# Low halves of attention keys in zero-padded 128-row tiles

## The chip, the cores and the metric

The kernel runs on one core of one Trainium2 chip. The metric is the device time of one execution in microseconds (us); lower is better. Three timed runs of the kernel before gave 2253.48, 2253.60 and 2255.27 us, the median is 2253.6 us.

The engines are called as the profile calls them: PE is the matrix engine (TensorE) and PEld its weight loads, DVE is VectorE, ACT is ScalarE, POOL is GpSimd, SP the engine that issues most DMAs. A matmul has a stationary operand, which a weight load puts into the array, and a moving operand, whose columns stream through it.

## The reference, cut to what matters

The model has two layers over 512 tokens of width 1024. A layer is a feed-forward block, a mixer and a second feed-forward block, all in float32.

```python
for l in range(DEPTH):
    h = h + 0.5 * swiglu(rms_norm(h, ffn1_norm[l]), ...)
    h = h + hybrid_mixer(rms_norm(h, mix_norm[l]), ...)
    h = h + 0.5 * swiglu(rms_norm(h, ffn2_norm[l]), ...)
```

The mixer has three kinds of heads of width 64: four heads of full attention that share two heads of keys and values, six heads of windowed attention with a bias by distance, and six heads of a gated delta rule that runs over the sequence in chunks of 64 tokens. The change touches the scores of the first two kinds, for one head `softmax(q k^T / 8 [+ bias])`, with 512 queries and 512 keys.

## The kernel before, in words

Every float32 matrix product that must be exact enough is split: an operand is rounded to a high half in the format fp32r, the rest is its low half, and products of halves are added up in PSUM. In the feed-forward blocks that is three matmuls of a 128x128 stationary tile with 512 moving columns (`mm3`, lines 214 to 218): high weights with high inputs, high weights with low inputs, low weights with high inputs. The first two have the same stationary operand, and each has its own weight load.

In attention two heads are a pair, called `tile_` in the code; there are five pairs in a layer and four blocks of 128 queries in each, so 20 units per layer. `queries` (line 812) makes for each head of the pair a tile `qs` of 128 rows: the 64 rows of the head's own half hold the high half of its queries, the other 64 rows hold the low half. `keys` (line 822) makes `kh`, in which head `i` has its high half twice, once in each half of the rows, so that one 128-row matmul adds high times high and low times high. The low half of the keys, `kl`, is one tile of 128 rows: rows 0 to 63 belong to the first head and rows 64 to 127 to the second.

`scores` (line 847) issues four matmuls for a unit. Two have the full `qs` block (128 rows) as stationary operand and `kh` as moving operand (line 863). Two have only the 64 rows with the high half of the queries as stationary operand, and 64 rows of `kl` as moving operand (line 865). DVE then finds the row minimum or maximum (with the bias added where there is one, line 876), ACT takes the exponential (line 873 or 878), DVE the reciprocal of the sum (line 879), and POOL scales the probabilities (line 880). `weigh` (line 884) runs one unit later: PE turns the probabilities (`ppt`, line 890, 128 rows and 128 columns of weights), ACT copies them (line 892), and PE multiplies them with the values (`pav`, line 896, 128 rows and 64 columns).

The scan of the delta rule is interleaved with the first fifteen units; its matmuls have 64-row or 64-column stationary operands (`pkq` line 685, `prr` line 697, `pS` line 707, `po` line 720). After unit 15 `delta_finish` (line 920) puts a run of small DVE operations beside the last units, and the output projection (`pwo`) begins between them.

The order of instructions on each engine is not that of the code alone: the kernel is built with a scheduler that orders them by its own model of their times, so an edit can move instructions it doesn't name. Each engine then runs its own list strictly in order, and waits on semaphores.

Memory of the attention pool lies on that of pools that were closed before. `delta_solve` and `project_groups` come just ahead of attention; `self.last` and `delta_solve` keep POOL busy until shortly before it.

Of the kernel before, what the change touches and what calls it, by code (L numbers as in the profile page):

```python
# [9 lines left out]
F32 = mybir.dt.float32  # L10
F32R = mybir.dt.float32r
# [8 lines left out]
P = 128  # L20
T = 512
# [330 lines left out]
class Mixer:  # L352
# [444 lines left out]
    def attention(self, ap, pp, scan, sp):  # L797
        k, nc, c = self.k, self.nc, self.c
        ident = c["ident"]
        self.mix = [None] * KD  # L800
        low, high = slice(0, 64), slice(64, 128)

        def gain(g, r):
            return g if isinstance(g, float) else g[r]

        def turned(qkv, tl):
            p = pp.tile([P, T], F32, name="pqk", tag="t", bufs=2)
            for t in range(NT):
                nc.tensor.transpose(out=p[:, t * P:t * P + P], in_=qkv[:, t, tl * P:tl * P + P], identity=ident)
            return p  # L810

        def queries(p, g):
            out = []
            for hb, other in ((low, high), (high, low)):
                q = ap.tile([P, T], F32R, name="qs", bufs=4)
                nc.scalar.activation(out=q[hb], in_=p[hb], func=AF.Copy, scale=gain(g, hb))
                nc.vector.scalar_tensor_tensor(out=q[other], in0=p[hb], scalar=gain(g, hb), in1=q[hb],
                                               op0=ALU.mult, op1=ALU.subtract)
                out.append(q)
            return out  # L820

        def keys(p, g):
            kh = ap.tile([P, 2, T], F32R, name="kh", bufs=2)
            kl = ap.tile([P, T], F32R, name="kl", bufs=2)
            for i, hb in enumerate((low, high)):
                for r in (low, high):
                    nc.scalar.activation(out=kh[r, i], in_=p[hb], func=AF.Copy, scale=gain(g, r))
                nc.vector.scalar_tensor_tensor(out=kl[hb], in0=p[hb], scalar=gain(g, hb), in1=kh[hb, i],
                                               op0=ALU.mult, op1=ALU.subtract)
            return kh, kl  # L830

        ops = {}

        def load(i):
            if i < 2:
                if i == 0:
                    kv = keys(turned(self.qkv[0], 2), 1.0), self.qkv[0][:, :, 384:512]
                else:
                    kv = ops[0][1:]
                ops[i] = (queries(turned(self.qkv[0], i), 0.125), *kv)  # L840
            elif i < 5:
                g = self.qkv[i - 1]
                ops[i] = (queries(turned(g, 0), self.gq8), keys(turned(g, 1), self.nbk), g[:, :, 256:384])

        state = {}

        def scores(tile_, t):
            if t == 0:
                state["pv"] = pp.tile([P, T], F32, name="pav", tag="v")
                state["bias"] = []  # L850
                if tile_ >= 2:
                    for h in (2 * tile_ - 4, 2 * tile_ - 3):
                        bias = ap.tile([P, NWIN], F32, name="bias", bufs=BIAS_BUFS)
                        src = k.line[h:h + 1, 0:P * 2 * T].rearrange("o (p n) -> (o p) n", n=2 * T)
                        nc.sync.dma_start(out=bias, in_=src[:, P - 1:P - 1 + NWIN])
                        state["bias"].append(bias)
            if t == LOAD_AT:
                load(tile_ + 1)
            tk = slice(t * P, t * P + P)
            q, (kh, kl), v = ops[tile_]  # L860
            ps = [pp.tile([P, T], F32, name="psc", tag="s", bufs=2) for _ in range(2)]
            for par in range(2):
                nc.tensor.matmul(out=ps[par], lhsT=q[par][:, tk], rhs=kh[:, par], start=True, stop=False)
            for par, hb in enumerate((low, high)):
                nc.tensor.matmul(out=ps[par], lhsT=q[par][hb, tk], rhs=kl[hb], start=False, stop=True)  # L865
            probs = []
            for par in range(2):
                pb = ap.tile([P, T], F32, name="prob", bufs=2 * AHEAD + 2)
                nm = ap.tile([P, 1], F32, name="nm", bufs=2 * AHEAD + 2)
                sm = ap.tile([P, 1], F32, name="sm", bufs=2 * AHEAD + 2)  # L870
                if tile_ < 2:
                    nc.vector.tensor_reduce(out=nm, in_=ps[par], axis=AX, op=ALU.max, negate=True)
                    nc.scalar.activation(out=pb, in_=ps[par], func=AF.Exp, bias=nm, accum_out=sm)
                else:
                    o = T - P - t * P
                    nc.vector.tensor_tensor_reduce(out=pb, in0=ps[par], in1=state["bias"][par][:, o:o + T], scale=1.0,
                                                   scalar=3e38, op0=ALU.add, op1=ALU.min, accum_out=nm)
                    nc.scalar.activation(out=pb, in_=pb, func=AF.Exp, scale=-1.0, bias=nm, accum_out=sm)
                nc.vector.reciprocal(out=sm, in_=sm)  # L879
                nc.gpsimd.tensor_tensor(out=pb, in0=pb, in1=sm.to_broadcast([P, T]), op=ALU.mult)  # L880
                probs.append(pb)
            return probs, state["pv"], v, tile_, t

        def weigh(probs, pv, v, tile_, t):
            tk = slice(t * P, t * P + P)
            turns = []
            for pb in probs:
                pt = pp.tile([P, T], F32, name="ppt", tag="t", bufs=2)
                for kt in range(NT):
                    nc.tensor.transpose(out=pt[:, kt * P:kt * P + P], in_=pb[:, kt * P:kt * P + P], identity=ident)  # L890
                full = ap.tile([P, T], F32, name="pth", bufs=4)
                nc.scalar.activation(out=full, in_=pt, func=AF.Copy)
                turns.append(full)
            for kt in range(NT):
                for hb, full in zip((low, high), turns):
                    nc.tensor.matmul(out=pv[hb, tk], lhsT=v[:, kt, hb], rhs=full[:, kt * P:kt * P + P],  # L896
                                     start=kt == 0, stop=kt == NT - 1)
            if t == NT - 1:
                hi = k.xp.tile([P, T], F32R, name="mxh", tag=f"xh{tile_}")
                lo = k.xp.tile([P, T], F32R, name="mxl", tag=f"xl{tile_}")  # L900
                nc.scalar.activation(out=hi, in_=pv, func=AF.Copy)
                nc.vector.tensor_tensor(out=lo, in0=pv, in1=hi, op=ALU.subtract)
                self.mix[tile_] = hi, lo

        pending = []
        load(0)
        for tile_ in range(5):
            for t in range(NT):
                pending.append(scores(tile_, t))
                if len(pending) > AHEAD:  # L910
                    weigh(*pending.pop(0))
                unit = 4 * tile_ + t
                for _ in range(SCAN_AT.count(unit)):
                    next(scan)
                if unit == FINISH_AT:
                    self.delta_finish(sp)
        for u in pending:
            weigh(*u)
# [136 lines left out]
```

## Time and profile before

| | |
|---|---|
| median of three timed runs | 2253.6 us |
| profiled execution, its span (the profile gives no other time of it) | 2258.2 us |
| PE busy | 2206.7 us, 98% |
| PEld busy | 1749.9 us, 77% |
| DVE busy | 1143.1 us, 51% |
| ACT busy | 789.7 us, 35% |
| POOL busy | 478.3 us, 21% |
| matmuls on line 863 (`kh`) | 80, mean 520 ns |
| matmuls on line 865 (`kl`) | 80, mean 530 ns |
| weight loads of lines 216 and 217, which share the stationary operand | 1408 each, mean 188 ns |

Busy time is the time in which an engine had some instruction under way; matmuls overlap, so the duration of one matmul is longer than the step from its start to the start of the next, and it is this step that says how fast PE gets on. The attention of layer 1 lies between about 590 and 724 us of the span, that of layer 2 between about 1712 and 1838 us. The granted clock of PE (PEclk) is 1.00 at its upper level of 2.4 GHz and 0.50 at 1.2 GHz.

### The profile page before, as it was taken

To read this page: it belongs to the slowest core of one execution; us is meant where nothing else is said; L and a number is where in the kernel's file an instruction comes from. 1 tells how busy PE (TensorE), PEld (TensorE's weight loads), DVE (VectorE), ACT (ScalarE), POOL (GpSimd) and SP (SyncE) were. 2 spreads that over 40 slices of the span, in tenths; PEclk is the share of its full clock that TensorE was granted. 3 is DMA by queue.
4 is the path that set the end of the run, shared out by engine and by line. 5 is a ranking of instruction groups with operands and counts; after the bars stand their busy time and mean duration, and the time that the engine had idled before them with its cause. 6 is when DMAs were issued, how large, how long until landed. Compare 5 with 4: busy or idle time off the path is not lost.

```text
span 2258.2 us, 30283 instructions
## 1 busy us (share of the span) xinstructions
PE 2206.7 (98%) x12212; PEld 1749.9 (77%) x12212; DVE 1143.1 (51%) x1881; ACT 789.7 (35%) x1153; POOL 478.3 (21%) x482
## 2 busy tenths in 40 slices
PE   8999999998999999999999999999989999999999
PEld 5888887778766888888788888877787778888887
DVE  5333334779567443333443333447795765434333
ACT  4222223534465332222332222235335643222221
POOL 3101012207154220101221010123072532101010
PEclk9999999999799999999999999999998999999999
DMA  5432323233202223333232323232341023232333
GB/s 174 123 96 96 97 92 124 75 92 98 57 18 81 92 92 96 94 91 101 85 95 91 102 91 97 91 124 68 100 111 36 28 94 93 94 93 92 95 94 102
DMA packets 93076, 206.82 MB, mean 92 GB/s; under 512 B 38561, under 2 KB 39073, under 8 KB 92936
## 3 DMA queue, kind: packets, MB, share of 16 engines
q1 hardware_dynamic: 91168, 199.98, 29.0%
q10 hardware_dynamic: 1768, 4.91, 0.7%
q8 instruction: 96, 1.57, 0.3%
q14 instruction: 44, 0.36, 0.1%
HBM read 193.83 MB, written 14.18 MB: 92 GB/s over the span
## 4 chain that ended last, share of the span: by engine, by line
PE 89%; DVE 7%; issue 1%; ACT 1%; DMA 1%; SPq 0%; ACTq 0%; DVEq 0%
PE pg L218 14%; PE pg L216 14%; PE pg L217 14%; PE pd L218 7%; PE pd L217 7%; PE pd L216 7%; PE pc L216 2%; PE pav L896 2%; PE ppt L890 2%; PE pc L218 2%; PE pc L217 2%; PE psc L865 1%; PE pkq L685 1%; PE pwo L217 1%; DVE wlo L211 1%
## 5 line engine op out<-in xcount | busy, mean ns | idle before, releaser
L210 ACT ACTIVATE whi<-wraw 128x1024 fp32r<-128x1024 f32 (+3 forms) x344 | 351.3, 1022 | 1225.7 <-PE pg L217 655.3
L216 PE MATMUL pg<-xh,whi 128*128 128x512 f32 x1408 | 558.2, 397 | 8.5 <-ACT xh L236 8.3
L217 PE MATMUL pg<-xl,whi 128*128 128x512 f32 x1408 | 558.7, 397 | 1.6 <-DVE xl L237 1.5
L218 PE MATMUL pg<-xh,wlo 128*128 128x512 f32 x1408 | 558.0, 396 | 0.8 <-DVE wlo L211 0.8
L211 DVE TENSOR_TENSOR wlo<-wraw,whi 128x1024 fp32r<-128x1024 f32 (+3 forms) x344 | 409.1, 1189 | 89.8 <-ACT whi L210 83.4
L296 POOL TENSOR_TENSOR s<-s,rstd 128x512 f32<-128x512 f32 x88 | 152.7, 1737 | 1146.5 <-ACT s L295 1146.5
L216 PEld LDWEIGHTS pg<-xh,whi 128*128 128x128 f32 x1408 | 265.4, 188 | 73.4 <-ACT xh L236 8.3
L217 PEld LDWEIGHTS pg<-xl,whi 128*128 128x128 f32 x1408 | 265.1, 188 | 68.0 <-DVE xl L237 4.8
L218 PEld LDWEIGHTS pg<-xh,wlo 128*128 128x128 f32 x1408 | 265.3, 188 | 65.2 <-DVE wlo L211 1.9
L218 PE MATMUL pd<-hh,wlo 128*128 128x512 f32 x704 | 278.7, 396 | 0.9 <-DVE wlo L211 0.9
L216 PE MATMUL pd<-hh,whi 128*128 128x512 f32 x704 | 278.4, 396 | 0.0
L217 PE MATMUL pd<-hl,whi 128*128 128x512 f32 x704 | 278.4, 395 | 0.0
L310 DVE SCALAR_TENSOR_TENSOR x<-pd,x 128x512 f32<-128x512 f32 x96 | 66.4, 691 | 283.4 <-PE pd L218 283.4
L298 DVE TENSOR_TENSOR h<-pg,s 128x512 f32<-128x512 f32 x88 | 60.8, 691 | 287.9 <-PE pg L218 281.4
L294 DVE TENSOR_TENSOR s<-pg,rstd 128x512 f32<-128x512 f32 x88 | 60.6, 692 | 229.6 <-PE pg L218 229.5
L218 PEld LDWEIGHTS pd<-hh,wlo 128*128 128x128 f32 x704 | 132.3, 188 | 34.0 <-DVE wlo L211 2.2
L217 PEld LDWEIGHTS pd<-hl,whi 128*128 128x128 f32 x704 | 132.3, 188 | 31.9
L216 PEld LDWEIGHTS pd<-hh,whi 128*128 128x128 f32 x704 | 132.4, 188 | 31.8
L880 POOL TENSOR_TENSOR prob<-prob,sm 128x512 f32<-128x512 f32 x80 | 84.3, 1061 | 149.8 <-DVE sm L879 126.3
L753 PE MATMUL pgr<-wlo,xh 128*128 128x384 f32 (+1 forms) x256 | 91.4, 357 | 12.2 <-DVE wlo L211 12.1
L245 POOL TENSOR_TENSOR acc<-acc,sq 128x512 f32<-128x512 f32 x42 | 67.4, 1606 | 132.6 <-ACT sq L244 131.9
L754 PE MATMUL pgr<-whi,xl 128*128 128x384 f32 (+1 forms) x256 | 90.1, 352 | 0.0
(234 smaller groups left out, 2712.8 us busy)
## 6 DMA issues: line engine op xcount, KB each, us to landing
wraw<-in_gu_dram SPq DMA_DIRECT2D x176, 512.0 KB, 3.6
wraw<-in_wd_dram SPq DMA_DIRECT2D x64, 448.0 KB, 3.3
wraw<-in_wd_dram SPq DMA_DIRECT2D x32, 512.0 KB, 3.5
wraw<-in_w_c_dram SPq DMA_DIRECT2D x24, 512.0 KB, 3.6
wraw<-in_w_gb_dram SPq DMA_DIRECT2D x24, 384.0 KB, 3.0
wraw<-in_w_o_dram SPq DMA_DIRECT2D x14, 512.0 KB, 3.6
bias<-line SPq DMA_DIRECT2D x12, 448.0 KB, 4.9
saved<-x SPq DMA_DIRECT2D x16, 256.0 KB, 2.0
```

The lines of the kernel that those rows point to most:

```text
L210: nc.scalar.activation(out=hi, in_=raw, func=AF.Copy)
L211: nc.vector.tensor_tensor(out=lo, in0=raw, in1=hi, op=ALU.subtract)
L216: nc.tensor.matmul(out=out, lhsT=w[0], rhs=x[0], start=first, stop=False)
L217: nc.tensor.matmul(out=out, lhsT=w[0], rhs=x[1], start=False, stop=False)
L218: nc.tensor.matmul(out=out, lhsT=w[1], rhs=x[0], start=False, stop=last)
L245: nc.gpsimd.tensor_tensor(out=n["acc"], in0=n["acc"], in1=sq, op=ALU.add)
L296: nc.gpsimd.tensor_tensor(out=s, in0=s, in1=n["rstd"], op=ALU.mult)
L298: nc.vector.tensor_tensor(out=h, in0=pp[1], in1=s, op=ALU.mult)
L310: nc.vector.scalar_tensor_tensor(out=self.x[dm], in0=p, scalar=0.5, in1=self.x[dm], op0=ALU.mult, op1=ALU.add)
L753: nc.tensor.matmul(out=o, lhsT=xh[:, tk], rhs=lo[:, wc], start=False, stop=False)
L754: nc.tensor.matmul(out=o, lhsT=xl[:, tk], rhs=hi[:, wc], start=False, stop=kk == KD - 1)
L880: nc.gpsimd.tensor_tensor(out=pb, in0=pb, in1=sm.to_broadcast([P, T]), op=ALU.mult)
```

## The change

`kl` becomes a tile of 128 rows for each head, as `kh` is: head `i` writes its low half into the 64 rows where its high queries lie, and the other 64 rows are zero. The matmul on `kl` then takes the full 128-row `qs` block as stationary operand, the same as the matmul on `kh`; the low queries meet the zeros. To write the zeros only once per layer, two such tiles (`pads`) are made at the start of attention, zeroed by four memsets on POOL, and used in turn. Each tile is 4 KB per row, where `kl` had 2 KB.

```diff
+        kept, pads = [], [ap.tile([P, 2, T], F32R, name=f"kl{i}") for i in range(2)]
+        for kl in pads:
+            for i, other in enumerate((high, low)):
+                nc.gpsimd.memset(kl[other, i].bitcast(F32), 0.0)
...
-            kl = ap.tile([P, T], F32R, name="kl", bufs=2)
+            kl = pads[len(kept) % 2]
+            kept.append(kl)
...
-                nc.vector.scalar_tensor_tensor(out=kl[hb], in0=p[hb], scalar=gain(g, hb), in1=kh[hb, i],
+                nc.vector.scalar_tensor_tensor(out=kl[hb, i], in0=p[hb], scalar=gain(g, hb), in1=kh[hb, i],
...
             for par in range(2):
                 nc.tensor.matmul(out=ps[par], lhsT=q[par][:, tk], rhs=kh[:, par], start=True, stop=False)
-            for par, hb in enumerate((low, high)):
-                nc.tensor.matmul(out=ps[par], lhsT=q[par][hb, tk], rhs=kl[hb], start=False, stop=True)
+                nc.tensor.matmul(out=ps[par], lhsT=q[par][:, tk], rhs=kl[:, par], start=False, stop=True)
```

The number of matmuls and weight loads stays as it is. The order moves at a few places. On PE near the end of the attention of layer 1 (`ppt` are turned probabilities, `pwo` the output projection), this stood before:

```order
L890 MATMUL ppt<-consts,prob 128x128 x4
L863 MATMUL psc<-kh,qs 128x512 x2
L896 MATMUL pav<-pth,qkv_4426 64x128
L865 MATMUL psc<-kl,qs 128x512 x2
L890 MATMUL ppt<-consts,prob 128x128 x4
```

and the same stretch has these rows now:

```order
L894 MATMUL ppt<-consts,prob 128x128 x4
L868 MATMUL psc<-kh,qs 128x512
L869 MATMUL psc<-kl_4637,qs 128x512
L216 MATMUL pwo_6223<-mxh,wohi_6218 128x512
L217 MATMUL pwo_6223<-mxl,wohi_6218 128x512
L868 MATMUL psc<-kh,qs 128x512
L869 MATMUL psc<-kl_4637,qs 128x512
L900 MATMUL pav<-pth,qkv_4426 64x128 x7
```

Two `kl` matmuls of 64 rows that stood side by side are apart, each now right behind its `kh` matmul. Before there are three places with two `kl` side by side, now there is none.

On PE at the opening of the attention of layer 2, behind the first `prr` of the scan, this stood before:

```order
L697 MATMUL prr<-vs,Y_11917 64x64
L863 MATMUL psc<-kh,qs 128x512
L865 MATMUL psc<-kl,qs 128x512
L707 MATMUL pS<-vn,kd_12008 64x64 x6
L707 MATMUL pS<-vn,kd_12009 64x64 x6
L720 MATMUL po<-vn,A_11918 64x64
```

and this stands now:

```order
L697 MATMUL prr<-vs,Y_11919 64x64
L707 MATMUL pS<-vn,kd_12010 64x64 x6
L707 MATMUL pS<-vn,kd_12011 64x64 x6
L720 MATMUL po<-vn,A_11920 64x64
L720 MATMUL po<-vn,A_11921 64x64
L720 MATMUL po<-vn,A_11920 64x64
L720 MATMUL po<-vn,A_11921 64x64
L720 MATMUL po<-vn,A_11920 64x64
L868 MATMUL psc<-kh,qs 128x512
L869 MATMUL psc<-kl_13385,qs 128x512
```

The first pair of score matmuls has moved behind the scan's `pS` and part of its `po`; that is the order which layer 1 has in both kernels.

On POOL at the opening of the attention of layer 1, the state of the scan is cleared and scaled (`S`), and the first probabilities follow. Before:

```order
L625 TENSOR_TENSOR yi_3532<-yi_3532,tmp_3534 96x30
L669 MEMSET S 128x768
L713 TENSOR_TENSOR S<-S,lstep 64x6x64 x2
L880 TENSOR_TENSOR prob<-prob,sm 128x512
L713 TENSOR_TENSOR S<-S,lstep 64x6x64 x2
```

and now:

```order
L625 TENSOR_TENSOR yi_3532<-yi_3532,tmp_3534 96x30
L669 MEMSET S 128x768
L713 TENSOR_TENSOR S<-S,lstep 64x6x64 x2
L805 MEMSET kl_4636 64x512 x2
L805 MEMSET kl_4637 64x512 x2
L884 TENSOR_TENSOR prob<-prob,sm 128x512
L713 TENSOR_TENSOR S<-S,lstep 64x6x64 x2
```

The four memsets stand between the scaling of `S` and the first probabilities. The first two wait for DMAs of `delta_solve` whose memory they take; the other two wait for the last `pp` matmul of `delta_solve` (line 658). Only the first two are waited for by the first score matmuls on `kl`. On SP the order of DMAs is unchanged.

## Rows read from the trace of the kernel before

**Rows 1.** The page: the chain of work that ended last, by engine.
```profile
PE 89%; DVE 7%; issue 1%; ACT 1%; DMA 1%; SPq 0%; ACTq 0%; DVEq 0%
```

**Rows 2.** Busy us of each engine by stretch, PEclk, DMA share, GB/s.
```profile
617.00:703.00 86.00, 83.47 (x956) 60.11 (x954) 57.40 (x134) 52.95 (x109) 44.58 (x45) 1.00 0.06 19
703.00:724.00 21.00, 19.54 (x164) 13.32 (x163) 18.47 (x54) 11.77 (x26) 9.12 (x8) 1.00 0.09 26
1818.00:1838.00 20.00, 20.00 (x181) 14.37 (x177) 16.80 (x52) 11.70 (x27) 9.36 (x8) 1.00 0.10 28
```

**Rows 3.** Waits of PE, 590 to 724 us: us in total, times, longest.
```profile
PE pav L896 <- ACT pth L892: 1.3, 1, 1.3
```

**Rows 4.** Line 865 alone by stretch: PE and PEld busy, PEclk, DMA, GB/s.
```profile
586.00:617.00 31.00, 4.75 (x6) 1.71 (x6) 0.50 0.01 2
617.00:703.00 86.00, 13.45 (x28) 4.93 (x28) 1.00 0.06 19
703.00:724.00 21.00, 2.48 (x6) 0.92 (x6) 1.00 0.09 26
1709.00:1726.00 17.00, 2.38 (x3) 0.86 (x3) 0.50 0.00 1
1726.00:1818.00 92.00, 15.90 (x33) 5.85 (x33) 1.00 0.05 17
1818.00:1838.00 20.00, 1.99 (x4) 0.73 (x4) 1.00 0.10 28
```

**Rows 5.** Lines 863 and 865: ns min/median/max, starts; idle before.
```profile
L863 PE MATMUL psc<-kh,qs x80: 387/495/796, 593.5 to 1827.8; 128*128 128x512 f32 x80
...
L865 PE MATMUL psc<-kl,qs x80: 490/498/793, 594.2 to 1828.2; 64*128 64x512 f32 x80
...
  issue: 21.0, 77
```

**Rows 6.** Timeline of PE, 700 to 716 us: start, us, line, tiles, count.
```profile
703.01 0.49 PE L865 MATMUL psc<-kl,qs 64*128 64x512 f32 x2
...
706.70 0.50 PE L865 MATMUL psc<-kl,qs 64*128 64x512 f32 x1
707.13 0.49 PE L863 MATMUL psc<-kh,qs 128*128 128x512 f32 x1
...
708.78 0.39 PE L218 MATMUL pwo<-mxh,wolo 128*128 128x512 f32 x1
709.02 0.39 PE L216 MATMUL pwo<-mxh,wohi 128*128 128x512 f32 x1
...
709.70 0.39 PE L216 MATMUL pwo<-mxh,wohi 128*128 128x512 f32 x1
710.02 1.09 PE L896 MATMUL pav<-pth,qkv 128*64 128x128 f32 x16
711.05 0.50 PE L217 MATMUL pwo<-mxl,wohi 128*128 128x512 f32 x1
711.38 0.39 PE L218 MATMUL pwo<-mxh,wolo 128*128 128x512 f32 x1
```

**Rows 7.** Timeline of weight loads, same stretch, idle time ahead in brackets.
```profile
707.55 0.18 PEld L865 LDWEIGHTS psc<-kl,qs 64*128 64x128 f32 x1 [0.24 <-issue]
...
708.79 0.19 PEld L216 LDWEIGHTS pwo<-mxh,wohi 128*128 128x128 f32 x1
```

**Rows 8.** Timeline, 580 to 606 us, in the low clock.
```profile
598.85 0.79 PE L865 MATMUL psc<-kl,qs 64*128 64x512 f32 x1
...
599.57 1.55 PE L685 MATMUL pkq<-S,kq 128*64 128x128 f32 x8
```

**Rows 9.** Timelines around the opening of attention in layer 1, POOL and PE.
```profile
561.12 0.74 POOL L669 MEMSET S<- 128x768 f32 x1 [5.73 <-ACT xi L631]
...
598.03 1.04 POOL L880 TENSOR_TENSOR prob<-prob,sm 128x512 f32<-128x512 f32 x1 [33.57 <-DVE sm L879]
...
585.96 2.47 PE L658 MATMUL pp<-Y,p1s 32*32 32x32 f32 x48 [0.90 <-ACT p1s L653]
```

## The prediction

> **What bounds the kernel now.** I read the chain of waits first. PE holds 89% of it [rows 1], so what shortens PE's list can shorten the kernel. Then busy time by stretch, for the two stretches in which the change lies. In most of the attention of layer 1 PE is busy for 83.47 of 86 us and DVE for 57.40; in its last 21 us DVE is busy for 18.47, nearly as much as PE's 19.54, and at the end of layer 2 for 16.80 of 20 [rows 2]. Then who waits for whom: over the whole attention of layer 1 PE's longest entry is one wait of 1.3 us for ACT [rows 3], and the list has six entries with 4.7 us in all. So attention is bound by PE, except for its two tails, where a run of small DVE operations could be the limit. Last the timeline of PE and of its weight loads, to see what a step on PE costs. There the reader is to look at starts, not at durations: a `kl` matmul lasts 0.498 us and a `kh` matmul 0.495 us in the median [rows 5], but the step from one start to the next is what counts.
>
> **What a step costs.** Where matmuls of 128 rows and 128 weight columns follow each other, the step is 0.24 us (708.78 to 709.02) [rows 6]; others of that run are 0.23. I take 0.23. When the next one has another form (64 of rows or columns), the step is 0.32 (709.70 to 710.02). The step of the first one behind such a switch is 0.33 (711.05 to 711.38). One between two switches takes both: `kl` to `kh` is 0.43 (706.70 to 707.13) [rows 6]. So a change of form costs 0.09 us on the way in and 0.10 behind it, 0.19 together. The loads show why: the load for 709.02 starts at 708.79, while the matmul of 708.78 runs; the load of a `kl` matmul comes only after 0.24 us in which PEld did nothing [rows 7], and over all `kl` loads that idle time is 21.0 us in 77 places [rows 5]. The number of rows by itself costs nothing: with 64 rows and with 128 the 512 columns take the same time.
>
> The Trainium skill says the same of the switch: in "TensorEngine Tiling (Array Packing)", Key Properties, changing the tiling mode drains the engine. It also holds a rule against the change (Tiling Modes there): two tiles of 64 rows work at once. The trace agrees where two stand side by side: at 703.01 two `kl` matmuls share 0.49 us [rows 6]. By that rule alone, with all 40 units so ordered, padding would cost 40 steps of 0.23, 9.2 us; the order has only three such places, and the sum below goes by these.
>
> **The sum.** Removed:
> - In PE's order before, 77 of the 80 `kl` matmuls stand behind another form (74 of them behind `kh`), the other three behind a `kl`. The switch ahead of each of the 77 goes: 77 x 0.09 = 6.9 us, and the step behind it loses its 0.10: 7.7 us. 14.6 together.
> - 38 of them have a 128x128 matmul next (`kh`, `ppt`, `pqk`, `pwo`), 42 in the new order. The switch back goes as well: 42 x 0.19 = 8.0 us. For the other 38 the next matmul has 64 rows or columns, and that switch stays.
> - Nine of the 80 lie in the low clock [rows 4], where the step of 0.43 is 0.72 (598.85 to 599.57) [rows 8]. At that ratio of 1.67 their share gains 9/80 x 22.6 x 0.67 = 1.7 us more.
>
> Added:
> - Three pairs that ran side by side now take a step each: 3 x 0.23 = 0.7 us.
> - Four memsets per layer on POOL. A memset of 768 columns took 0.74 us; 512 columns are 0.49 in proportion, 2 us for the four. POOL lies idle for 33.57 us ahead of 598.03 [rows 9]. The first two, which the score matmuls wait for, wait for DMAs ahead of that idle time; the second two wait for the `pp` matmuls that end at about 588.4 (585.96 + 2.47) and end some 1 us later, 8 us ahead of POOL's next work. Cost 0 for both layers; without that cover at most the 2 us per layer, and below nothing it can't be.
> - Weight loads: one for each matmul as before. That two matmuls share a stationary operand saves none; the FFN's pairs with the same weights have one load each as well.
> - DVE writes the same number of columns for `kl`. A padded tile of zeros streams the same 512 columns.
>
> So PE's list gets 14.6 + 8.0 + 1.7 - 0.7 = 23.6 us shorter, about 24.
>
> What of it shows in the time? Ten of the 80 `kl` matmuls lie in the two tails [rows 4], where DVE is nearly as full as PE [rows 2]; I take nothing there, which leaves 70/80, 21 us. In the rest PE would be 21 us faster over some 225 us, so waits for DVE, ACT and POOL that now end early enough will sometimes end last: `ppt` for POOL's probabilities, `pkq` and `pS` for the scan on DVE, `kh` and `qs` at the start of a pair of heads. The bound is from no such loss (21 us) to half (10 us). As PE waits so little now [rows 3] I take a fifth, 4 us. Then 17 us remain.
>
> The profiled span of 2258.2 us is 4.6 us, 0.2%, longer than the median of the timed runs; I take the difference over unchanged: 2253.6 - 17 = 2236.6, say 2237 us.
>
> **The clock.** It falls to the low level ahead of both attentions, while PE runs short matmuls of 32 rows with gaps, and rises again in them: 31 us at 0.50 in layer 1, 17 us in layer 2 [rows 4]. One us at the low level does the work of 0.6 us (0.43 against 0.72), so it loses 0.40. Fuller matmuls with fewer gaps may bring the rise earlier; the opening of layer 2 now has layer 1's order, in which the rise came 14 us later, worth 14 x 0.40 = 5.6 us of loss. I can't tell which is stronger and put 0 into the forecast, from -6 to +6 into the range.
>
> **The rivals.**
> - *The clock rises earlier.* If layer 1 recovers in the 17 us of layer 2, 5.6 us more are gained: 2231. If both come still earlier, 2226. For it: `kl` steps leave less time between columns. Against it: most of the opening is scan work that doesn't change.
> - *The gain is eaten.* Layer 2 recovers as late as layer 1 does now (5.6 us), or waits on DVE and POOL take half of 21 us instead of a fifth: 17 - 6 = 11 us gained, 2243; with both, 2248. For it: the reordering above, DVE's load in the tails. Against: PE's few waits.
> - *No change.* The second load of the same rows waits for the matmul ahead as the load of `kl` does now, so a padded `kl` steps as a `kl` does: 0.43 remains, 2253 to 2254. "TensorE: Matmul & The Clock Gate" in the Trainium skill, Part 3, says that a load overlaps with matmuls under way only where the row groups differ, which would give this. The trace speaks against it: the load at 708.79 runs beside the matmul of 708.78, both of 128 rows [rows 7, 6].
> - *Slower.* The low clock holds on. If the opening runs on with scan and scores so mixed that the rise comes later in both layers, each us costs 0.40; the 17 us are used up after 17/0.40 = 43 us more of low clock, and it is slower by over 0.2% after 54 us, that is 27 us in each layer: 2258 or more. Nothing in the trace shows so late a rise.
>
> **How the numbers follow.** The forecast has 0.55, the earlier clock 0.20, the eaten gain 0.15, no change 0.05, slower 0.05. What can be told from no change is about 0.2%, 4.5 us. Faster by more than that are the first three nearly in full, 0.89; within it 0.06; slower 0.05. The forecast's own range is 2231 to 2243. For 8 in 10 I go down into the earlier clock, to 2226, and up into the eaten gain, to 2248.
>
> **What would show it.** Right: the padded matmul starts 0.23 us behind `kh` where that follows its own form, and 0.33 behind a switch; its load has no idle time for "issue" ahead; PE is still what ends last between the opening and the tail; the memsets end ahead of the first `kl` matmul. The forecast is wrong if the step stays at 0.43; if PE's waits in attention rise far over the 4 us per execution allowed for; or if the stretches at 0.50 are much longer or shorter than 31 and 17 us.

## The result, and the profile after

The changed kernel takes 2238.26 us in the median of six runs, against 2255.44 us for six runs of the kernel before (the three known ahead and three more). One of the six runs of the changed kernel, which took 8773.61 us at a granted clock of 1.00, counts in its median but not in the ratio. The ratio on record is 0.9904, 95% interval 0.9879 to 0.9929; it is not the quotient of the two medians, which is 0.9924. The forecast was 2237 us. The profiled execution has a span of 2232.6 us, 25.6 us less than that of before, so it shows more gain than the medians do; the paragraph on the clock says why.

The page of the changed kernel: span, busy time of each engine, and the chain of work that ended last.

```profile
span 2232.6 us, 30294 instructions
...
PE 2179.1 (98%) x12212; PEld 1745.9 (78%) x12212; DVE 1138.8 (51%) x1881; ACT 789.5 (35%) x1153; POOL 483.7 (22%) x490
...
PE 88%; DVE 8%; ACT 2%; issue 1%; DMA 1%; POOL 0%; ACTq 0%; SPq 0%; DVEq 0%; POOLq 0%
```

PE held 89% of the chain [rows 1] and holds 88%: it is still the bound, with a list that takes 27.6 us less of busy time (2206.7 before).

Busy time by stretch (PE, PEld, DVE, ACT, POOL, then PEclk, DMA share and GB/s). The attention of layer 1 now lies between 590 and 711 us.

```profile
598.00:686.00 88.00, 84.54 (x1065) 66.12 (x1062) 63.89 (x152) 59.47 (x124) 51.77 (x52) 1.00 0.06 18
686.00:711.00 25.00, 22.79 (x196) 16.34 (x194) 22.47 (x61) 15.85 (x32) 9.57 (x9) 1.00 0.25 75
```

The stretch between the opening and the tail had 956 matmuls in 86 us [rows 2], 11.1 per us; now it has 1065 in 88, 12.1 per us. This compares only roughly, as the stretch now begins earlier in PE's list. DVE did not become the bound there. In the tail DVE is busy for 22.47 of 25 us, about as full as before.

Waits of PE between 590 and 711 us (total, times, longest):

```profile
PE pkq L685 <- DVE S L715: 1.1, 2, 0.5
PE prr L697 <- ACT Y L662: 1.1, 1, 1.1
...
PE pwo L217 <- DVE mxl L952: 0.9, 1, 0.9
```

No entry is above 1.1 us; before, the longest was 1.3 [rows 3]. All idle time of PE in the two attentions together rose from 12.4 to 14.8 us.

The two lines of the score matmuls (ns min/median/max, starts; idle time ahead):

```profile
L868 PE MATMUL psc<-kh,qs x80: 389/478/793, 594.5 to 1801.6; 128*128 128x512 f32 x80
...
  issue: 2.7, 16
...
L869 PE MATMUL psc<-kl,qs x80: 387/396/628, 595.1 to 1801.9; 128*128 128x512 f32 x80
```

The 21.0 us of "issue" in 77 places ahead of the `kl` loads [rows 5] are gone; line 869 has no idle time at all, and `kl` lasts 396 ns in the median instead of 498. The steps show what that is worth. Timeline of PE (start, us):

```profile
689.78 0.48 PE L868 MATMUL psc<-kh,qs 128*128 128x512 f32 x1
690.10 0.40 PE L869 MATMUL psc<-kl,qs 128*128 128x512 f32 x1
690.43 1.09 PE L900 MATMUL pav<-pth,qkv 128*64 128x128 f32 x14
...
692.75 0.48 PE L868 MATMUL psc<-kh,qs 128*128 128x512 f32 x1
693.07 0.39 PE L869 MATMUL psc<-kl,qs 128*128 128x512 f32 x1
693.30 0.39 PE L218 MATMUL pwo<-mxh,wolo 128*128 128x512 f32 x1
693.53 0.39 PE L216 MATMUL pwo<-mxh,wohi 128*128 128x512 f32 x1
```

Read the starts: `kl` to `pwo`, both of the full form, 0.23 us; `kl` to `pav`, a change of form, 0.33. Before, `kl` to `kh` took 0.43 [rows 6], and the medians of `kl` to `pwo` and `kl` to `pav` were 0.42 and 0.43. The weight loads of the same places:

```profile
692.73 0.19 PEld L868 LDWEIGHTS psc<-kh,qs 128*128 128x128 f32 x1
692.84 0.19 PEld L869 LDWEIGHTS psc<-kl,qs 128*128 128x128 f32 x1
693.07 0.19 PEld L218 LDWEIGHTS pwo<-mxh,wolo 128*128 128x128 f32 x1
```

The load for `kl` starts at 692.84, while the `kh` matmul of 692.75 runs; before it came after 0.24 us of nothing [rows 7]. Both use all 128 rows. The rule of "TensorE: Matmul & The Clock Gate" in the Trainium skill, Part 3, that loads overlap only where the row groups differ, doesn't hold for this pair.

POOL ahead of attention (idle time and what ended it in brackets):

```profile
567.28 1.09 POOL L805 MEMSET kl<- 64x512 f32 x2 [1.23 <-DMA s<-xi]
...
589.54 1.09 POOL L805 MEMSET kl<- 64x512 f32 x2 [21.16 <-PE pp L658]
599.31 1.04 POOL L884 TENSOR_TENSOR prob<-prob,sm 128x512 f32<-128x512 f32 x1 [8.68 <-DVE sm L883]
```

The memsets last 0.55 us each and end at 590.6, 4.5 us ahead of the first `kl` matmul (595.1) and 8.7 us ahead of POOL's next work.

Line 869 by stretch, the opening of each attention and what follows (PE and PEld busy, PEclk, DMA, GB/s):

```profile
588.00:598.00 10.00, 0.63 (x1) 0.33 (x1) 0.50 0.01 2
598.00:686.00 88.00, 13.51 (x34) 6.61 (x35) 1.00 0.06 18
...
1694.00:1704.00 10.00, 0.63 (x1) 0.33 (x1) 0.50 0.01 2
```

Here something is new: the stretch at the lower level, 31 and 17 us before [rows 4], is 10 us in both layers of this execution.

**Two measures for the experiments.** The first is the *step sum*: over all matmuls in the two attentions, from the first `prr` to the first `pwo` on `whi`, the time from one start to the next, less 0.40 us for each us at the lower level. It tells what PE's list and its waits cost at the full clock. With it goes the number of *changes of form*, places in PE's executed list where rows or columns of the stationary operand differ from those of the matmul before. The second is the *time at equal clock*. Each timed run has its span and its mean granted clock; twice what the clock lacks to 1, times the span, is its time at the lower level. In 69 runs of the kernel before that time lies between 31.5 and 86.4 us, mean 55.6, and the run's time follows it along a line: 2241.8 us plus 0.39 us for each us, with 1.1 us of scatter about it. (The clock is on record to three digits, so for one run this time is known to within 2.3 us.) The distance of a kernel's runs from this line is what it changes apart from the clock.

| kernel | changes of form | step sum, us | time at equal clock, us | lower level, mean of runs, us | median, us | ratio |
|---|---|---|---|---|---|---|
| before, page above | 332 | 252.1 | 0 | 55.6 | | |
| e9, before again | 332 | 252.3 | +0.1 | 56.6 | 2262.52 | 1.0000 [0.9977, 1.0022] |
| e1, changed again | 214 | 234.4 | -16.8 | 33.5 | 2238.78 | 0.9893 [0.9872, 0.9913] |
| e4, other stationary | 214 | 234.3 | -17.7 | 40.3 | 2241.05 | 0.9900 [0.9882, 0.9919] |
| e2, full-attention pairs | 283 | 250.5 | -1.4 | 44.0 | 2257.37 | 0.9978 [0.9963, 0.9992] |
| e3, windowed pairs | 264 | 243.2 | -9.9 | 64.7 | 2257.89 | 0.9979 [0.9963, 0.9995] |
| e5, 64 rows, side by side | 274 | 243.9 | -10.4 | 52.2 | 2252.08 | 0.9951 [0.9939, 0.9963] |
| e6, no `kl` | 222 | 222.1 | -27.1 | 40.1 | 2228.92 | 0.9856 [0.9840, 0.9872] |
| e7, memsets four times | 229 | 239.0 | -13.2 | 48.7 | 2247.95 | 0.9932 [0.9918, 0.9946] |
| e8, filler matmuls | 219 | 242.4 | -3.9 | 19.5 | 2246.61 | 0.9923 [0.9907, 0.9938] |
| e10, values padded too | 121 | 258.1 | +3.0 | 46.0 | 2263.48 | 0.9988 [0.9974, 1.0003] |
| e11, four side by side | 226 | 250.4 | -4.6 | 40.5 | 2253.12 | 0.9946 [0.9927, 0.9966] |

The changed kernel itself has 214 and 234.2. But for e8, whose fillers lie ahead of the first `prr`, the two measures agree within 3 us in each row. The count alone does not set the sum: e2 has 49 changes of form less than the kernel before and e11 106 less, and their step sums are only 1.6 and 1.7 us shorter.

### The profile page after: what moved, and what is told of

Read it like the earlier page. It is cut to its first block, busy times and chain, and to the rows that moved or that the text cites. A ratio compares the mean times of both kernels' runs of the same rounds, so it can differ in the third digit from the quotient of the medians.

```text
span 2232.6 us, 30294 instructions
## 1 busy us (share of the span) xinstructions
PE 2179.1 (98%) x12212; PEld 1745.9 (78%) x12212; DVE 1138.8 (51%) x1881; ACT 789.5 (35%) x1153; POOL 483.7 (22%) x490
## 4 chain that ended last, share of the span: by engine, by line
PE 88%; DVE 8%; ACT 2%; issue 1%; DMA 1%; POOL 0%; ACTq 0%; SPq 0%; DVEq 0%; POOLq 0%
PE pg L218 15%; PE pg L216 15%; PE pg L217 15%; PE pd L218 7%; PE pd L216 7%; PE pd L217 7%; PE pc L216 2%; PE pc L218 2%; PE pc L217 2%; PE pav L900 1%; PE ppt L894 1%; DVE wlo L211 1%; PE pwo L217 1%; PE pwo L216 1%; PE pwo L218 1%
## 5 line engine op out<-in xcount | busy, mean ns | idle before, releaser
L296 POOL TENSOR_TENSOR s<-s,rstd 128x512 f32<-128x512 f32 x88 | 152.7, 1737 | 1146.5 <-ACT s L295 1146.5
L753 PE MATMUL pgr<-wlo,xh 128*128 128x384 f32 (+1 forms) x256 | 92.0, 360 | 11.2 <-DVE wlo L211 11.1
```

Source lines behind the costliest of these rows:

```text
L296: nc.gpsimd.tensor_tensor(out=s, in0=s, in1=n["rstd"], op=ALU.mult)
L753: nc.tensor.matmul(out=o, lhsT=xh[:, tk], rhs=lo[:, wc], start=False, stop=False)
```

## The experiments

**e1, the changed kernel again** (no edit), as the partner of the runs beside it.

> The changed kernel once more, beside the others of this call. Theory: 2235 to 2240 us, 15 to 20 us below the kernel before, with two short stretches of low clock (about 10 us each) in the two attentions, where the kernel before has 31 and 17. If the earlier rise of the clock was a chance of one execution, the low stretches come out near 31 and 17 us again and the gain is only that of the steps, some 17 us less 4.

Its step sum is that of the first profile within 0.2 us, its time within 0.6 us. What it gains at equal clock is 16.8 us. The stretches at the lower level are 17 and 14 us long, not about 10 as expected, but they begin earlier: 7.6 and 9.7 us after the first `prr` PE is back at 1.00, as in the first profile (7.6 and 7.2).

**e2 and e3, half of the change each.** In e2 only the four full-attention heads (pairs 0 and 1, which also open the attention) have padded low halves, in e3 only the six windowed ones.

```diff
-            kl = pads[len(kept) % 2]
+            wide = isinstance(g, float)          # e3: not isinstance(g, float)
+            kl = pads[0] if wide else ap.tile([P, T], F32R, name="ks", bufs=2)   # e3: pads[len(kept) % 2], bufs=1
...
+                if wide:
+                    nc.tensor.matmul(out=ps[par], lhsT=q[par][:, tk], rhs=kl[:, par], start=False, stop=True)
+                else:
+                    nc.tensor.matmul(out=ps[par], lhsT=q[par][hb, tk], rhs=kl[hb], start=False, stop=True)
```

> Only the low keys of the full-attention heads are padded: the first two of five pairs of heads, 32 of the 80 matmuls on kl, all of those in the openings. Theory (a change of form costs 0.19 us, and fuller openings bring the clock's rise forward): 32/80 of the 17 us of the steps is 7, and all of the clock's part, 20 us less of low clock at 0.40, 8 us: about 2240, with low stretches near 10 us. Rival (the clock's rise does not come from the padding): 7 us only, about 2247, low stretches near 31 and 17 us.

> The other part: only the low keys of the windowed heads are padded, 48 of the 80 matmuls on kl, none in the openings. Theory: 48/80 of 17 us is 10, and nothing of the clock: about 2244, low stretches near 31 and 17 us. Rival (the clock's rise does not come from the padding): low stretches as short as in the changed kernel, about 2236.

The halves gain 5 us each in the median, the whole 24: not additive, and both theories and both rivals missed. The two measures take this apart. e3 gains its 10 us of steps, and 4.5 us of them go to the clock (64.7 us at the lower level against 53.1 in the mean of the kernel before in this series, at 0.39); e2 has the better clock and few of the steps. In e2 the 32 padded `kl` and their `kh` do step faster (`kl` 0.31 us in the mean, 0.43 for the 48 of 64 rows), but PE idles for 18.4 us in the attentions instead of 12.4, and `pav` and `pwo` cost 2.8 and 2.0 us more. The opening of layer 2, PE busy and PEclk, first of e2:

```profile
1711.00:1718.00 7.00, 5.90 (x76) 0.53 0.01 2
1718.00:1737.00 19.00, 19.00 (x218) 1.00 0.01 2
```

and of e3, whose opening has the 64-row `kl` of the kernel before:

```profile
1709.00:1718.00 9.00, 8.28 (x86) 0.50 0.01 2
1718.00:1736.00 18.00, 18.00 (x122) 0.50 0.00 1
```

In e2 PE is back at 1.00 from 1718 us on, 4 us behind its first scores (1713.6). In e3, whose first scores start at 1712.4, it stays at 0.50 for 18 us more, although PE is busy for all of them. Over 12 timed runs of each, the lower level takes 44.0 us in e2 and 64.7 in e3. The order of this opening does not explain it: e2 has the first scores ahead of `pS`, as the kernel before has them, and e3 has them behind it, as the changed kernel has.

**e4, the same form with another stationary operand.** The `kl` matmul takes another block of 128 queries than its `kh`.

```diff
+            other = slice((3 - t) * P, (3 - t) * P + P)
-                nc.tensor.matmul(out=ps[par], lhsT=q[par][:, tk], rhs=kl[:, par], start=False, stop=True)
+                nc.tensor.matmul(out=ps[par], lhsT=q[par][:, other], rhs=kl[:, par], start=False, stop=True)
```

> The changed kernel, but the second score matmul of a head takes another block of 128 queries as stationary operand, of the same form (the low part of the scores is then that of other queries). Theory (the form alone counts, every matmul loads its weights anyway): the same time as the changed kernel within 3 us, 2235 to 2240. Rival (the shared stationary operand saves part of the load): up to 0.10 us for each of 80, 8 us slower, about 2246.

Step sum 234.3 against 234.4 of e1, the time within the overlap of both. So that the two matmuls share the operand shows no gain here (the 2.3 us between the medians go with the clock: 40.3 us against 33.5 at the lower level is 2.7 at 0.39); the shared form gives it.

**e5, the order instead of the padding.** The kernel before, with both 64-row `kl` matmuls of a unit held behind its second `kh`; 39 of 40 pairs then stand side by side.

```diff
-                nc.tensor.matmul(out=ps[par], lhsT=q[par][:, tk], rhs=kh[:, par], start=True, stop=False)
-            for par, hb in enumerate((low, high)):
-                nc.tensor.matmul(out=ps[par], lhsT=q[par][hb, tk], rhs=kl[hb], start=False, stop=True)
+                last = nc.tensor.matmul(out=ps[par], lhsT=q[par][:, tk], rhs=kh[:, par], start=True, stop=False)
+            with self.tc.issue_after(last.ins):
+                for par, hb in enumerate((low, high)):
+                    nc.tensor.matmul(out=ps[par], lhsT=q[par][hb, tk], rhs=kl[hb], start=False, stop=True)
```

> The kernel before with nothing padded: the two kl matmuls of a unit are held behind the second kh matmul, so that in 39 of 40 units they stand side by side and take one step together. Theory (changes of form cost, and two 64-row matmuls side by side share a step): 58 changes of form fewer than before and 36 shared steps of 0.23 us more, at most 11 + 8 us of steps; as in the changed kernel about four fifths show, 15 us. With openings that are not padded the low clock stays as erratic as before (10 to 28 us in each attention): 2240 to 2252. Rival (side by side they don't share): 7 us at most, 2250 or more.

Timeline of PE in e5:

```profile
646.42 0.50 PE L866 MATMUL psc<-kl,qs 64*128 64x512 f32 x2
646.85 0.66 PE L891 MATMUL ppt<-consts,prob 128*128 128x128 f32 x4
...
661.42 0.50 PE L866 MATMUL psc<-kl,qs 64*128 64x512 f32 x2
663.30 0.63 PE L891 MATMUL ppt<-consts,prob 128*128 128x128 f32 x4 [1.38 <-DVE qs L817]
```

Two `kl` of 64 rows share one step of 0.43, as the three pairs of the kernel before did. "TensorEngine Tiling (Array Packing)" in the Trainium skill, Tiling Modes, has that right. So `kl` as a whole costs 22.2 us, a little less than the 23.3 of the padded ones. But `kh` keeps a change of form behind it and costs 29.5 instead of 24.8, and holding `kl` back for its partner adds waits: PE idles for 20.0 us in the attentions instead of 12.4. The gain at equal clock is 10.4 us, against 17 for padding. The time of 2252.08 us lies at the upper end of what the theory gave.

**e6, no `kl` matmuls,** the changed kernel without the low half of the keys (it isn't added to the scores).

```diff
-                nc.tensor.matmul(out=ps[par], lhsT=q[par][:, tk], rhs=kh[:, par], start=True, stop=False)
-                nc.tensor.matmul(out=ps[par], lhsT=q[par][:, tk], rhs=kl[:, par], start=False, stop=True)
+                nc.tensor.matmul(out=ps[par], lhsT=q[par][:, tk], rhs=kh[:, par], start=True, stop=True)
```

> The changed kernel without the matmuls on kl (the low half of the keys is left out of the scores). Theory (PE bounds attention, and a padded kl matmul costs its step of 0.29 us on average): 80 x 0.29 = 23 us less than the changed kernel, about 2215; some of it is eaten by waits for DVE and POOL, so 2215 to 2222. Rival (by now other engines bound attention): less than half of it, 2227 or more.

It takes 2228.92 us. Of the 23.3 us that the padded `kl` steps cost, 12.1 go. The rest comes back, `kh` first (5.9 us), then `ppt` (2.3) and `po` (2.2). Timeline of PE in e6:

```profile
645.10 0.48 PE L868 MATMUL psc<-kh,qs 128*128 128x512 f32 x1
645.50 0.92 PE L697 MATMUL prr<-t,Y 64*64 64x64 f32 x24
```

`kh` now meets the change of form itself, a step of 0.40 where it had 0.23 to 0.34 with a padded `kl` behind it. Leaving out 80 matmuls is worth 10 us more than padding them. The time is that of the rival, but its reason, that other engines bound attention, is the smaller part: PE's idle time rose by 3.2 us, from 14.8 to 18.0, while `kh` alone, with the change of form behind it, takes back 5.9.

**e7, each memset four times.**

```diff
-                nc.gpsimd.memset(kl[other, i].bitcast(F32), 0.0)
+                for _ in range(4):
+                    nc.gpsimd.memset(kl[other, i].bitcast(F32), 0.0)
```

> The changed kernel with every memset made four times, 16 per layer. Theory (POOL lies idle there): the first eight end some 20 us ahead of the first kl matmul, the others about 4 us ahead of POOL's next work: no change, 2235 to 2241. Rival (the memsets or their waits hold something up): 12 more memsets of 0.54 us in each layer show, up to 13 us, 2251.

It is 9 us slower than e1: 3.6 us at equal clock, and 5.9 by 15.2 us more at the lower level. "No change" missed. POOL ahead of attention in e7:

```profile
565.73 1.09 POOL L806 MEMSET kl<- 64x512 f32 x2 [1.28 <-DMA s<-xi]
588.20 7.97 POOL L806 MEMSET kl<- 64x512 f32 x14 [21.37 <-PE pp L658]
```

Only the first two memsets run early; the other 14 wait for `pp`, six of them for the first tile. The scheduler moved the score matmuls with them. PE in e7:

```profile
593.17 0.79 PE L869 MATMUL psc<-kh,qs 128*128 128x512 f32 x1
597.95 0.80 PE L869 MATMUL psc<-kh,qs 128*128 128x512 f32 x1
599.44 0.74 PE L870 MATMUL psc<-kl,qs 128*128 128x512 f32 x2
```

The first `kl` start 4.3 us later than in the changed kernel (595.1), `kh` and `kl` are split, and the list has 15 more changes of form. So memsets cost nothing while they are four short ones; the cover is not as wide as POOL's idle time looks.

**e8, filler matmuls,** to keep PE's clock up: 8 matmuls of the full form, whose results nobody reads, behind each of the last two rounds of `pp` in a layer (`marks` are the last matmuls of these rounds, `FILL` is 4).

```diff
...
+            if tile_ == 0 and t == 0:
+                x = self.n["x"][7][0]
+                for mark in self.marks:
+                    with self.tc.issue_after(mark.ins):
+                        for j in range(2 * FILL):
+                            nc.tensor.matmul(out=ps[j % 2], lhsT=x[:, 0:P], rhs=x, start=True, stop=True)
```

> The changed kernel with 16 matmuls of 128x128x512 that nobody reads, in each layer just ahead of the attention, eight on either side of the last pp matmuls, where PE waits for ACT. Theory (the clock falls because PE has gaps and small matmuls there): the low stretch is gone or shorter; 15 us of low clock less is 6 us gained, the fillers cost 7.4 us less the 4 us of waits that they fill: about 2235. If the clock falls all the same, 3 us slower than the changed kernel, about 2241.

PE in e8:

```profile
589.89 3.78 PE L874 MATMUL psc<-xh 128*128 128x512 f32 x8
593.60 1.91 PE L659 MATMUL pp<-Y,p1s 32*32 32x32 f32 x48
595.43 2.11 PE L874 MATMUL psc<-xh 128*128 128x512 f32 x8
```

The time at the lower level falls to 19.5 us, 14 below e1, worth 14 x 0.39 = 5.5 us; the fillers themselves hold PE for 3.71 + 2.04 us in layer 1 and 3.16 + 2.04 in layer 2, 11.0 in both. Net 5.5 us lost by this sum, 7.8 measured; PE's idle time in the attentions, 18.3 us instead of 14.8, is part of the rest. Theory and rival both missed: the lower level got shorter, and the kernel is slower still.

**e9, the kernel before again** (no edit).

> The kernel before, unchanged, for another look at the clock in the openings of attention. Theory A (unpadded openings recover late and by chance): 10 to 45 us at the lower level in the two attentions together, where the padded kernels of the earlier runs had 15 to 19; step sums without the low clock again about 252 us with 332 changes of form. Rival (the short low stretches of the changed kernel were chance): below 20 us here too, with a time near 2245. Time by A: 2250 to 2262, ratio 1.000 within 0.002.

The step sum is 252.3, as in the first profile, and the rival (below 20 us at the lower level) is out. The opening of layer 2 in e9, PE busy and PEclk:

```profile
1712.00:1722.00 10.00, 7.20 (x114) 0.50 0.01 4
1722.00:1730.00 8.00, 8.00 (x70) 0.50 0.00 0
1730.00:1737.00 7.00, 7.00 (x23) 0.50 0.00 0
1737.00:1747.00 10.00, 10.00 (x105) 0.71 0.01 2
```

The lower level lasts past 1737 us. In the two attentions together it is 45.9 us here and 41.6 in the first profile of before, 30.2 in e5 and 37.9 in e3, all with 64-row `kl` in the opening. The kernels with padded openings have 14.8, 17.3, 15.1, 19.3 (e2), 24.6 (e7), 18.0 and 17.1 (e10, e11). In the timed runs it is the same: means of 52.2 to 64.7 us with 64-row openings (before, e9, e3, e5), 33.5 to 48.7 with padded ones (e1, e4, e2, e7, e10, e11). These means are the weaker evidence, as they count the whole span: in the profile of e4, 29 of 44 us at the lower level lie outside the attentions. Opening by opening, padded ones are back at 1.00 between 6.2 and 11.2 us after the first `prr` (one of e7's falls again, until 16.8). Those with 64 rows take 14 to 27 us in before and e9, but e3's first takes 9.7, with the same first matmuls that take 28.2 in its second layer, and e5's two take 10.2 (it falls again, until 17.0) and 9.7. So a long lower level goes with 64-row scores in the opening, yet not in every one of them. That the form is the cause is likely and not shown, and neither is how it would act.

**e10, the same idea on the values.** Not in the cut: the calls of the new copy, and `BIAS_BUFS`, which goes from 4 to 3 for room.

```diff
+        vals, wide = [], [ap.tile([P, NT, 192], F32, name=f"vz{i}") for i in range(2)]
+        for vz in wide:
+            nc.gpsimd.memset(vz[:, :, 64:128], 0.0)
...
+            for i, hb in enumerate((low, high)):
+                nc.gpsimd.tensor_copy(out=vz[:, :, P * i:P * i + 64], in_=v[:, :, hb])
...
-                    nc.tensor.matmul(out=pv[hb, tk], lhsT=v[:, kt, hb], rhs=full[:, kt * P:kt * P + P],
-                                     start=kt == 0, stop=kt == NT - 1)
+                    nc.tensor.matmul(out=pv[:, tk], lhsT=v[:, kt, 64 * i:64 * i + P], rhs=full[:, kt * P:kt * P + P],
+                                     start=kt == 0 and i == 0, stop=kt == NT - 1 and i == 1)
```

> The changed kernel with the values zero-padded as well: POOL copies each head's 64 columns of values into a tile with 64 columns of zeros between the two heads, and the 8 pav matmuls of a unit take 128 weight columns and add both heads up in one 128-row result; BIAS_BUFS is 3 for room. Full tiles and others change places 134 times in PE's list in the two attentions instead of 194. Theory A (each change of form costs 0.15 to 0.2 us, and a padded pav steps as the 64-column one does, 0.064 us a record): 9 to 12 us faster than the changed kernel, some 2227. Rival (two pav of 64 columns side by side share their time, and the padded ones step as pqk does, 0.09 us): 640 x 0.026 = 17 us more, less 9 to 12: 5 to 8 us slower than the changed kernel, some 2245.

The rival held, and by more than it asked: 93 changes of form less than the changed kernel, and yet 20 us slower at equal clock. PE in e10, then in the changed kernel:

```profile
663.90 1.72 PE L910 MATMUL pav<-pth,vz 128*128 128x128 f32 x14
665.46 0.60 PE L904 MATMUL ppt<-consts,prob 128*128 128x128 f32 x4
```

```profile
644.62 1.09 PE L900 MATMUL pav<-pth,qkv 128*64 128x128 f32 x14
645.64 0.66 PE L894 MATMUL ppt<-consts,prob 128*128 128x128 f32 x4
```

14 records take 1.56 us padded and 1.02 not. Inside a run a padded `pav` steps 0.112 us in the median, and two unpadded ones together take 0.109: the 64-column matmuls of the two heads stand side by side already and share their time. By the means, 0.115 and 0.067 us, that would be 31 us lost over 640 records; `pav` as a whole, its changes of form included, costs 73.1 instead of 54.1 us. Waits rose too: PE idles for 17.8 us.

**e11, all four score matmuls of a unit side by side,** by holding the first head's two behind the second's.

```diff
-            for par in range(2):
-                nc.tensor.matmul(out=ps[par], lhsT=q[par][:, tk], rhs=kh[:, par], start=True, stop=False)
-                nc.tensor.matmul(out=ps[par], lhsT=q[par][:, tk], rhs=kl[:, par], start=False, stop=True)
+            nc.tensor.matmul(out=ps[1], lhsT=q[1][:, tk], rhs=kh[:, 1], start=True, stop=False)
+            last = nc.tensor.matmul(out=ps[1], lhsT=q[1][:, tk], rhs=kl[:, 1], start=False, stop=True)
+            with self.tc.issue_after(last.ins):
+                nc.tensor.matmul(out=ps[0], lhsT=q[0][:, tk], rhs=kh[:, 0], start=True, stop=False)
+                nc.tensor.matmul(out=ps[0], lhsT=q[0][:, tk], rhs=kl[:, 0], start=False, stop=True)
```

> The changed kernel with the second head's kh and kl first and the first head's two held behind them, so that the four score matmuls of a unit stand side by side. Full tiles and others change places 198 times instead of 194. Theory A (the count of changes of form sets the gain): no difference from the changed kernel within 0.2%, 2234 to 2243, step sum 234 to 236. Rival (what counts is that a padded kl stands behind its own form; more of them in a row bring more, 40 places x 0.19): 7 us faster, 2231.

Both theories missed: it keeps 4.6 us of the 17 at equal clock. PE in e11:

```profile
659.17 0.40 PE L870 MATMUL psc<-kh,qs 128*128 128x512 f32 x1
659.41 0.40 PE L871 MATMUL psc<-kl,qs 128*128 128x512 f32 x1
661.22 0.92 PE L697 MATMUL prr<-t,Y 64*64 64x64 f32 x24 [1.41 <-DVE t L689]
662.75 0.63 PE L896 MATMUL ppt<-consts,prob 128*128 128x128 f32 x4 [0.62 <-DVE qs L821]
```

The steps inside the group are 0.24, and then PE waits 1.41 and 0.62 us for DVE. The median step of each kind is that of the changed kernel; PE's idle time in the attentions is 23.1 us instead of 14.8. Set against the mean step without a wait, about 10 of the 16 us by which the step sum is longer than the changed kernel's lie at the waits. This is the rival "the gain is eaten" of the prediction, made by an order that bunches the scores.

## Why the prediction was right, point by point

**The size of a step: right.** Medians of the steps outside the lower level, from one start to the next:

| step | before | after |
|---|---|---|
| `kh` to `kl`, `kh` behind `ppt` | 0.405 | 0.316 |
| `kh` to `kl`, `kh` behind `pav` | 0.432 | 0.335 |
| `kl` to `ppt` | 0.429 | 0.232 |
| `kl` to `pav` | 0.427 | 0.327 |

The forecast had 0.43 going to 0.23 within the form and 0.33 behind a switch, 0.09 in and 0.10 behind. One sign missed: behind a `ppt`, which has its own form, `kh` to `kl` was to be 0.23 and is 0.316 in 24 places (behind `kl` it is 0.233). The last section shows that the `ppt` ahead steps the less for it.

**The count: right.** 119 changes of form were to go (77 and 42); 332 became 214, which is 118.

**The sum: right within an us, in part by errors that cancel.** The step sum fell by 17.9 us: `kl` from 33.1 to 23.3, `kh` from 32.8 to 24.8, `ppt` by 2.1, `pqk` by 0.6; `pav` rose by 2.6, 1.7 of it in the wait for DVE ahead of `pot` (the turned output of the delta rule) in the tails. Without the share of the low clock the list was to be 22.6 - 0.7 = 21.9 us shorter. Taking PE's 2.4 us of added idle time off, it became 20.3 shorter. The allowances for tails (3 us) and waits (4 us) were too large, and the terms a little too, so two errors stand against each other in the 17. At equal clock five runs of the changed kernel lie 17.8 to 19.4 us below the line, those of e1 16.8 in the mean, against 17 in the forecast.

**Memsets at nothing, nothing from the shared operand: right** (589.54 + 1.09 ends ahead of 595.1; e4). e7 shows that the first of the two has a limit.

**The rival "no change": refuted.** The load of `kl` waits for nothing.

**The clock: mis-sized.** It stood at 0 in the forecast, with -6 to +6. In the attentions the lower level went from 41.6 to 14.8 us, 10.7 us at 0.40; over the whole spans, with three short stretches elsewhere that were not there before, from 47.8 to 30.7, 6.7 us at 0.39. With the 17.9 us of steps that makes 24.6 of the 25.6 us between the two profiles. So the argument that the opening of layer 2 would now recover as late as layer 1 did was wrong: after the first `prr` both recover sooner (7.6 and 7.2 us) than either did (27.4 and 14.2). What happened is the rival "the clock rises earlier", to which the prediction gave 0.20; its times of 2226 to 2231 did not come. The median came to the forecast all the same, because the three runs from which it started, 2253.5 to 2255.3 us, were runs with little of the lower level: by the line, 30 to 34 us, of 31.5 to 86.4 seen in all. That is luck: a gain left out and a start that was low by about as much. In the series of e1 the kernel before takes 2262.8 us in the mean and the changed one 2238.2; of these 24.6 us, (53.1 - 33.5) x 0.39 = 7.6 are the clock, a little beyond the -6 of the range. The price itself, 0.40 for each us, worked out from one pair of steps, is the 0.39 of 69 runs.

## What to carry to other kernels

Count the changes of form in PE's list, and look at the steps from start to start around them: padding a matmul with zeros to its neighbours' form paid where it stood alone between full tiles, 0.15 us for each change that went here, waits counted. It didn't pay where half-size matmuls already ran side by side, as `pav` did; and an order made by holding matmuls back added 8 us of idle time on PE, in e5 as in e11. Before a difference of less than 1% is read, look how the time of one and the same kernel follows the granted clock, and compare at equal clock.

## What the runs showed of the hardware that was not expected

- The time at the lower clock differs between executions of one kernel, from 31.5 to 86.4 us in 69 runs, and with it the time, from 2253.7 to 2275.2 us. PE at full busy time did not end it at once: in e9 it stayed at 0.50 from 1722 to 1737 us with PE busy for 15 of 15 us, with 64-row `kl` matmuls at 1724.25, 1726.74, 1732.18 and 1735.42 among others.
- Where `ppt` precedes a `kh` of its own form, the last `ppt` steps 0.028 us and the `kh` 0.316, together as much as 0.109 and 0.235. Single steps there tell little; the sum over neighbours does.
- Two 64-column `pav` in a row take 0.109 us together in the median, one of 128 columns takes 0.112: two heads side by side run there at twice the rate, as two 64-row `kl` sharing 0.43 us do.
